# Attention scores with joined products, an earlier square root and another order of the projections, in a two-layer hybrid decoder on one core

## The chip, the core and the metric

The kernel runs on one core of a Trainium2 chip. The core has a matrix engine (TensorE, PE in the profile, with its weight loads as PEld), a vector engine (VectorE, DVE), an activation engine (ScalarE, ACT), GpSimd (POOL), and SyncE (SP), which here issues the loads. The metric is the device time of one execution in microseconds, and the median of several executions is compared.

## The reference

Two layers, 256 tokens, width 1024. A layer adds four things to the residual stream: half of a gated feed-forward network, a mixing block, half of a second feed-forward network, and a gated per-layer input. The change lies in the mixing block. From one normalized input it computes two branches and merges them:

```python
rx, rgate, q, k, v, f_logit, ga, gb = jnp.split(proj, split_idx, axis=-1)
rx = causal_dwconv(rx, conv_w[i], conv_b[i])
ya = rg_lru(rx, rg_wa[i], rg_ba[i], rg_wx[i], rg_bx[i], rg_lambda[i])
ya = (ya * jax.nn.gelu(rgate)) @ w_rnn_out[i]
yb = forgetting_attention(q, k, v, f_logit, f_b[i], q_norm[i], k_norm[i]) @ w_attn_out[i]
merged = jax.nn.sigmoid(ga + mb_a) * ya + jax.nn.sigmoid(gb + mb_b) * yb
x = x + merged @ w_o[i]
```

The recurrent branch `rg_lru` is a gated linear recurrence over the tokens: `a = exp(log_a)`, `u = sqrt(-expm1(2 log_a)) * (i * x)`, and `h[t] = a[t] h[t-1] + u[t]`. The attention has 8 heads of 128 dimensions and two blocks of 128 queries. To each score it adds a forget bias, the cumulated log forget gate of the query less that of the key, ahead of the causal mask and the softmax:

```python
s = jnp.einsum('bhqd,bhkd->bhqk', qb, kh).astype(jnp.float32) * scale
s = s + dqb[..., None] - dcum[:, :, None, :]
s = jnp.where(kpos[None, :] <= qpos[:, None], s, -jnp.inf)
pr = jax.nn.softmax(s, axis=-1).astype(vh.dtype)
```

The query's part of the bias is the same for all keys of a row.

## The kernel before

All activations lie with the features on the 128 partitions and the 256 tokens along the row. Every float32 operand of a large product is split into a high part, rounded to the matrix engine's fp32r format, and a low part, the rest. A product of two such operands takes three fp32r products: high times high, high times low and low times high.

**Weights.** The class `Weights` walks a plan, a list of loads in the order of their use. `_emit` issues a load on SyncE (1 MB, three raw buffers) and splits it in units of mostly 128x1024: ScalarE writes the high part (L95), VectorE the low part (L96). `next` hands out a unit and keeps four further ones split ahead (`ahead=4`, five buffers).

**Order.** The program is written once in a wished order; the framework's scheduler then orders each engine's instructions by a simulated timeline and by program order. Buffers of one tag form a ring. Small pieces of work are put off with `defer` and are taken up by `tick`, one step at a time, between products.

**The mixing block `mix`** goes through these stages:

1. Eight products for the recurrent input (`rx_post`): each is scaled by the norm and convolved over four tokens.
2. Values and forget logits (`v`), eight weight units. Between them `gates(m)` runs the products of the recurrence's two gates, with the follow-up steps `s1` (decay, its square) and `s2` (the square under the root in `tq`, the input in `xc`).
3. Queries and keys: four groups of four units, `qk_group(cb, w)`, `cb` being the half of the heads and `w` query or key. In `during0`, which runs after each unit of the first two groups, the last three `gates` and the generator `forget` are put in. `forget` computes the log forget gate, cumulates it with a triangular product into `dps` and splits it. After the second group come `drain` and `root`: one square root over all eight tiles (L570) and a tiny exponential that brings back the other activation table (L572).
4. In `during1`, after each unit of the third group, two calls of `scan` (multiply L575, recurrence L576). In the fourth group the first steps of attention start.
5. Twenty-four `filler` projections of 24 products of 256 columns each (L304 to L306): eight for the gelu gate (`f < KT`), eight for merge gate A, eight for merge gate B. A gelu filler has five VectorE operations behind it (L759, L763, L767, L768 and the split), a merge gate filler one (L759). The fillers use a ring of four PSUM banks ("mm"); their evictions take buffers from a ring of twelve ("w").
6. The merge: per pair of output tiles two products with `wro` (tiles `ya`) and two with `wao` (tiles `yb`), then the output projection.

**Attention** has four steps per head, put into slots that `attend(i)` runs. Slots 0 to 7 belong to the units of groups three and four, slots 8 to 31 to the 24 fillers. Head h starts at slot 4 + (5h+1)//2, and each step comes a slot later than the one before. `step_a` transposes queries and keys (L693), splits them into five buffers of a ring of five ("aq"), one of them a bias operand that ScalarE makes for each head (L702). `step_b` makes the scores in one PSUM bank: for the first query block three products over 128 keys and a bias product (L711), for the second the same over 256 keys. The bias product has rows for the high and low part of the query's bias and of the key's. Then come the masked minimum (L715), the exponential (L717) and the division (L719, L721). `step_c` transposes the probabilities (L729) and splits them, `step_d` multiplies by the values (L739, L741) and splits the result into `ot`. PSUM banks of attention form a second ring of four ("at").

Of the kernel before, what the change touches and what calls it, by code (L numbers as in the profile page):

```python
# [16 lines left out]
P = 128  # L17
# [3 lines left out]
S = 256  # L21
# [23 lines left out]
WARM = 9  # L45
MF, MA, MB, MO = 6, 8, 2, 6


# [71 lines left out]
def trunk(ctx: ExitStack, tc: tile.TileContext, head, xT, pT, vec, w1i, w1o, wf, wqk, wv, wg, wro, wao, wo, w2i, w2o,  # L120
# [39 lines left out]
    for l in range(DEPTH):  # L160
        plan += [(w1i[l, j], [1024, 1024]) for j in range(2 if l == 0 else 0, FT)]
        plan += [(w1o[l, m, :, h * 1408:(h + 1) * 1408], [768, 640]) for m in range(KT) for h in range(2)]
        plan += [(wf[l, 0, c], [1024, 1024]) for c in range(4)]
        plan += [(wv[l, c], [4 * VC, 4 * VC]) for c in range(4)]
        plan += [(wqk[l, qk, cb, hf], [1024, 1024]) for cb in range(2) for qk in range(2) for hf in range(2)]
        plan += [(wf[l, f, c], [1024, 1024]) for f in (1, 2, 3) for c in range(4)]
        plan += [(wrao, [1024, 1024]) for c in range(4) for wrao in (wro[l, c], wao[l, c])]
        plan += [(wo[l, c], [1024, 1024]) for c in range(4)]
        plan += [(w2i[l, j], [1024, 1024]) for j in range(FT)]
        plan += [(w2o[l, m, :, h * 1408:(h + 1) * 1408], [768, 640]) for m in range(KT) for h in range(2)]  # L170
        plan += [(wpg[l, c], [1024, 1024]) for c in range(4)]
# [30 lines left out]

    acol = cp.tile([P, NH], F32, name="acol")
    mcol = cp.tile([P, NH], F32, name="mcol")
    grp = cp.tile([P, 4], F32, name="grp")
    sel = cp.tile([P, 3], F32, name="sel")
    lfh = cp.tile([P, TT, P], F32R, name="lfh")
# [26 lines left out]
    def constants():  # L234
# [12 lines left out]
        yield  # L247
        V.tensor_tensor(out=acol, in0=ident[:, 0:NH], in1=ident[:, 32:32 + NH], op=ALU.add)
        V.tensor_tensor(out=mcol, in0=ident[:, 64:64 + NH], in1=ident[:, 96:96 + NH], op=ALU.add)
        V.tensor_scalar(out=mcol, in0=mcol, scalar1=-1.0, scalar2=None, op0=ALU.mult)  # L250
        yield
        for g in range(4):
            V.tensor_reduce(out=grp[:, g:g + 1], in_=ident[:, 32 * g:32 * g + 32], axis=AX.X, op=ALU.add)
        yield
        V.tensor_tensor(out=sel[:, 0:1], in0=grp[:, 1:2], in1=grp[:, 3:4], op=ALU.add)
        V.tensor_scalar(out=sel[:, 0:1], in0=sel[:, 0:1], scalar1=-1.0, scalar2=None, op0=ALU.mult)
        V.tensor_tensor(out=sel[:, 1:2], in0=grp[:, 0:1], in1=grp[:, 1:2], op=ALU.add)
        V.tensor_tensor(out=sel[:, 2:3], in0=grp[:, 2:3], in1=grp[:, 3:4], op=ALU.add)
        yield
# [243 lines left out]
    def mix(l, n, wgp):  # L503
# [42 lines left out]
        tq = big([P, KT, S], F32, "tq")  # L546

        def gates(m):
            ps = two[m % 2]("g")
# [14 lines left out]
            def s2():  # L564
                V.scalar_tensor_tensor(out=tq[:, m], in0=a2, scalar=1.0, in1=th, op0=ALU.add, op1=ALU.mult)
                V.scalar_tensor_tensor(out=xc[:, m], in0=thi, scalar=1.0, in1=xc[:, m], op0=ALU.add, op1=ALU.mult)
            defer(s1, s2)

# [5 lines left out]
        def scan(m):  # L574
            V.tensor_tensor(out=tq[:, m], in0=tq[:, m], in1=xc[:, m], op=ALU.mult)  # L575
            V.tensor_tensor_scan(out=xc[:, m], data0=at[:, m], data1=tq[:, m], initial=0.0, op0=ALU.mult, op1=ALU.add)  # L576
# [30 lines left out]

        dc = kp.tile([P, S], F32R, name=nm("dc"), tag="dc", bufs=1)
        dk = kp.tile([P, S], F32R, name=nm("dk"), tag="dk", bufs=1)

        def forget():
# [4 lines left out]
            for t in range(TT):  # L616
                oh = lfh[:, t].rearrange("p (g c) -> p g c", g=4)[:, :, 0:NH]
                ol = lfl[:, t].rearrange("p (g c) -> p g c", g=4)[:, :, 0:NH]
                V.tensor_copy(out=oh, in_=lf3[:, t].to_broadcast([P, 4, NH]))
                V.tensor_tensor(out=ol, in0=lf3[:, t].to_broadcast([P, 4, NH]), in1=oh.bitcast(F32), op=ALU.subtract)  # L620
            yield
# [7 lines left out]
            A.activation(out=dh, in_=dps[:, 0:S], func=AF.Copy)  # L629
            V.scalar_tensor_tensor(out=dc, in0=dh.bitcast(F32), scalar=sel[:, 0:1], in1=dps[:, 0:S], op0=ALU.mult,  # L630
                                   op1=ALU.add)
            V.tensor_scalar(out=dk, in0=dc.bitcast(F32), scalar1=sel[:, 1:2], scalar2=sel[:, 2:3], op0=ALU.mult,
                            op1=ALU.add)

# [45 lines left out]
        root()  # L680

# [5 lines left out]
        def step_a(h):  # L687
# [3 lines left out]
            for w in range(2):  # L691
                for t in range(TT):
                    T.transpose(ps[:, (w * TT + t) * P:(w * TT + t + 1) * P], qk[cb][:, w, t, hh * P:(hh + 1) * P], ident)  # L693
            s["q"] = qh, ql = awork(S, "aq", 5), awork(S, "aq", 5)
# [6 lines left out]
            V.scalar_tensor_tensor(out=kl, in0=ps[:, S:], scalar=g, in1=kh.bitcast(F32), op0=ALU.mult, op1=ALU.subtract)  # L701
            A.activation(out=s["b"], in_=dc.bitcast(F32), func=AF.Identity, scale=mcol[:, h:h + 1], bias=acol[:, h:h + 1])  # L702

        def step_b(h):
            s = st[h]
            (qh, ql), (kh, kl), bl = s["q"], s["k"], s["b"]
            ps = atbank("s")
            for t, o, nk in ((0, 0, P), (1, P, S)):
                q = slice(t * P, (t + 1) * P)
                mm3(ps[:, o:o + nk], qh[:, q], ql[:, q], kh[:, 0:nk], kl[:, 0:nk], True, False)  # L710
                T.matmul(ps[:, o:o + nk], lhsT=bl[:, q], rhs=dk[:, 0:nk], start=False, stop=True)  # L711
            sv = pr = awork(384, "pr", 2, F32)
            mx, rs = small(TT, "mx", "sa"), small(TT, "rs", "sa")
            for t, o, nk in ((0, 0, P), (1, P, S)):
                V.tensor_tensor_reduce(out=sv[:, o:o + nk], in0=ps[:, o:o + nk], in1=mask[:, S - nk:S], scale=1.0,  # L715
                                       scalar=3e38, op0=ALU.add, op1=ALU.min, accum_out=mx[:, t:t + 1])
# [318 lines left out]
```

## Time and profile before

| what | value |
|---|---|
| median of 3 runs | 1322.99 us (1322.97 to 1323.11) |
| profiled execution, its own time | 1323.63 us |
| its span, first to last instruction | 1321.8 us |
| instructions | 22442 |
| granted TensorE clock, mean | 0.997 |
| PE busy | 1311.8 us |
| DVE busy | 1076.1 us |
| ACT busy | 815.5 us |

A line of the timeline gives the start in us from the span's beginning, the duration, the engine, the line of the program, the operation and the tile written and tiles read, with partitions and elements. Matrix products are pipelined: their durations overlap, and the distance between two starts is what a product costs. A line of the groups gives a count, the busy time, the mean duration in ns, then the idle time of the engine ahead of such instructions and what ended it. A line of the windows gives for a stretch its length and the busy time of each engine.

### The profile page before, as it was taken

How to read it: one execution, taken by the hardware profiler on the slowest of the kernel's cores; microseconds unless marked ns; L12 is line 12 of the kernel's file. 1: busy time of each engine (PE TensorE's matmuls, PEld its weight loads, DVE VectorE, ACT ScalarE, POOL GpSimd, SP SyncE). 2: the span in 40 equal slices, each digit the busy share in tenths (PEclk: the TensorE clock that was granted, in tenths of full speed). 3: DMA queues.
4: the chain of work that ended last, by engine and by line, in shares of the span. 5: the costliest groups of instructions: out<-in, count | busy, mean ns of one | idle time of the engine just before them, and what ended most of it. 6: DMA issues, size and time to landing. Idle time of an engine off the chain costs nothing.

```text
span 1321.8 us, 22442 instructions
## 1 busy us (share of the span) xinstructions
PE 1311.8 (99%) x8610; PEld 1197.7 (91%) x8610; DVE 1076.1 (81%) x2142; ACT 815.5 (62%) x1470; POOL 34.1 (3%) x43
## 2 busy tenths in 40 slices
PE   9999999999999999999999999999999999999997
PEld 8888899889999888889988888998999998888897
DVE  7998769899757899876789877698997678988756
ACT  6665656868655666565566555578677556655653
POOL 1000000020000000000000000000200000000000
PEclk9999999999999999999999999999999999999998
DMA  8654665445435555456545546644543455554650
GB/s 292 243 179 160 212 225 193 158 164 175 151 128 191 196 189 189 162 184 231 187 165 192 188 153 212 241 161 159 193 166 128 161 190 191 192 191 142 213 187 33
DMA packets 37259, 240.21 MB, mean 182 GB/s; under 512 B 4128, under 2 KB 4768, under 8 KB 14368
## 3 DMA queue, kind: packets, MB, share of 16 engines
q1 hardware_dynamic: 36720, 238.25, 51.3%
q8 instruction: 68, 1.11, 0.3%
q10 hardware_dynamic: 432, 0.52, 0.1%
q14 instruction: 39, 0.32, 0.1%
HBM read 237.71 MB, written 1.05 MB: 181 GB/s over the span
## 4 chain that ended last, share of the span: by engine, by line
PE 99%; DMA 0%; DVE 0%; ACT 0%; SPq 0%; POOLq 0%; issue 0%; DVEq 0%
PE mm L347 20%; PE mm L345 11%; PE at L347 11%; PE at L345 6%; PE f L304 3%; PE f L305 3%; PE f L306 3%; PE qk L309 2%; PE qk L311 2%; PE qk L310 2%; PE mm L306 2%; PE mm L304 2%; PE mm L305 2%; PE ya L347 2%; PE mm L344 2%; PE at L344 2%
## 5 line engine op out<-in xcount | busy, mean ns | idle before, releaser
L95 ACT ACTIVATE wh<-wr 128x1024 fp32r<-128x1024 f32 (+2 forms) x476 | 467.4, 986 | 308.0 <-PE mm L347 90.8
L96 DVE TENSOR_TENSOR wl<-wr,wh 128x1024 fp32r<-128x1024 f32 (+2 forms) x476 | 537.7, 1132 | 142.3 <-ACT wh L95 136.9
L347 PE MATMUL mm<-h,wh 128*128 128x512 f32 x616 | 219.2, 394 | 0.0
L347 PE MATMUL at<-h,wh 128*128 128x512 f32 x616 | 218.4, 394 | 0.0
L345 PE MATMUL mm<-h,wl 128*128 128x256 f32 x704 | 182.4, 281 | 0.0
L345 PE MATMUL at<-h,wl 128*128 128x256 f32 x704 | 181.7, 281 | 0.3 <-DVE wl L96 0.2
L347 PE MATMUL mm<-f,wh 128*128 128x512 f32 x504 | 176.8, 394 | 0.0
L345 PE MATMUL mm<-f,wl 128*128 128x256 f32 x528 | 144.0, 280 | 0.0
L345 PEld LDWEIGHTS at<-h,wl 128*128 128x128 f32 x704 | 131.8, 188 | 8.8 <-DVE wl L96 0.8
L345 PEld LDWEIGHTS mm<-h,wl 128*128 128x128 f32 x704 | 131.8, 188 | 7.8 <-DVE wl L96 0.4
L347 PEld LDWEIGHTS mm<-h,wh 128*128 128x128 f32 x616 | 115.6, 188 | 22.5
L347 PEld LDWEIGHTS at<-h,wh 128*128 128x128 f32 x616 | 114.9, 188 | 21.9
L347 PEld LDWEIGHTS mm<-f,wh 128*128 128x128 f32 x504 | 94.4, 188 | 20.8
L304 PE MATMUL f<-h,wh 128*128 128x256 f32 x384 | 108.6, 283 | 0.0
L306 PE MATMUL f<-h,wl 128*128 128x256 f32 x384 | 108.4, 282 | 0.0
L305 PE MATMUL f<-h,wh 128*128 128x256 f32 x384 | 108.4, 282 | 0.0
L345 PEld LDWEIGHTS mm<-f,wl 128*128 128x128 f32 x528 | 99.4, 188 | 2.1
L305 PEld LDWEIGHTS f<-h,wh 128*128 128x128 f32 x384 | 72.3, 188 | 0.1
L304 PEld LDWEIGHTS f<-h,wh 128*128 128x128 f32 x384 | 72.3, 188 | 0.1
L306 PEld LDWEIGHTS f<-h,wl 128*128 128x128 f32 x384 | 72.4, 189 | 0.0
L381 ACT ACTIVATE sum<-mm 128x256 f32<-128x256 f32 x112 | 40.2, 376 | 49.3 <-PE mm L347 49.3
L382 DVE TENSOR_TENSOR sum<-mm,sum 128x256 f32<-128x256 f32 x112 | 44.9, 417 | 15.0 <-ACT sum L381 15.0
(291 smaller groups left out, 2857.6 us busy)
## 6 DMA issues: line engine op xcount, KB each, us to landing
wr<-in_w2i SPq DMA_DIRECT2D x44, 1024.0 KB, 4.8
wr<-in_w1i SPq DMA_DIRECT2D x41, 1024.0 KB, 4.8
wr<-in_wf SPq DMA_DIRECT2D x32, 1024.0 KB, 4.8
wr<-in_w1o SPq DMA_DIRECT2D x32, 704.0 KB, 4.0
wr<-in_w2o SPq DMA_DIRECT2D x32, 704.0 KB, 4.0
wr<-in_wqk SPq DMA_DIRECT2D x16, 1024.0 KB, 4.8
wr<-in_wv SPq DMA_DIRECT2D x8, 1032.0 KB, 4.9
wr<-in_wro SPq DMA_DIRECT2D x8, 1024.0 KB, 4.8
```

The source lines that it names most:

```text
L95: self.nc.scalar.activation(out=hi[:, c], in_=src[:, c], func=AF.Copy)
L96: self.nc.vector.tensor_tensor(out=lo[:, c], in0=src[:, c], in1=hi[:, c].bitcast(F32), op=ALU.subtract)
L304: T.matmul(ps, lhsT=wh, rhs=xh, start=first, stop=False)
L305: T.matmul(ps, lhsT=wh, rhs=xl, start=False, stop=False)
L306: T.matmul(ps, lhsT=wl, rhs=xh, start=False, stop=last)
L309: T.matmul(ps, lhsT=xh, rhs=wh, start=first, stop=False)
L310: T.matmul(ps, lhsT=xh, rhs=wl, start=False, stop=False)
L344: T.matmul(ps, lhsT=wh, rhs=t, start=True, stop=False, skip_group_check=True)
L345: T.matmul(ps[:, 0:S], lhsT=wl, rhs=t[:, 0:S], start=False, stop=False, skip_group_check=True)
L347: T.matmul(ps, lhsT=wh, rhs=t, start=False, stop=last, skip_group_check=True)
L381: A.activation(out=o, in_=ps[:, S:], func=AF.Copy)
L382: V.tensor_tensor(out=o, in0=ps[:, 0:S], in1=o, op=ALU.add)
```

## The change

The change has six parts.

- **Scores.** The high and low part of a head's key lie side by side in one buffer `ak`. Six products take the place of eight. Three run the second block's queries over 256 keys. One runs the first block's high queries over the high and the low key at once, 2 x 128 columns, into two pieces of the bank; one adds the first block's low queries. One product of 384 columns adds the bias to both blocks. VectorE adds the extra piece of the first block to the mask (`m0`, from the ring "w") ahead of the masked minimum.
- **Bias.** Only the key's part of the forget bias is added. `dk` holds its high and low rows over 256 keys and once more over the first 128. The weights of the bias product are one column of the selection matrix `pick`, read 128 times. The tile `dc`, the per-head bias operand on ScalarE, and the constants `acol`, `mcol`, `grp` and `sel` go; `neglo` and `pick` come.
- **Square root.** `root` moves from behind the second q/k group to the second unit of that group. The steps put off are taken up until all eight tiles are ready. `forget` is put off two units later.
- **Scans.** One scan follows each unit from there on, instead of two after each unit of the third group. Its multiplication stays behind the VectorE instruction written before it.
- **Projections in turn.** Two gelu fillers, then two of merge gate A, four times over; merge gate B last as before. The weights' plan follows that order.
- **Attention.** Its slots start at 8 (`AT0`) instead of 4.

```diff
-        plan += [(wf[l, f, c], [1024, 1024]) for f in (1, 2, 3) for c in range(4)]
+        plan += [(wf[l, f, c], [1024, 1024]) for c in range(4) for f in (1, 2)]
+        plan += [(wf[l, 3, c], [1024, 1024]) for c in range(4)]
...
+        V.tensor_tensor(out=pick, in0=ident[:, 0:NH], in1=ident[:, 32:32 + NH], op=ALU.add)
+        V.tensor_reduce(out=neglo, in_=ident[:, 32:64], axis=AX.X, op=ALU.add)
+        V.tensor_scalar(out=neglo, in0=neglo, scalar1=-1.0, scalar2=None, op0=ALU.mult)
...
         def scan(m):
-            V.tensor_tensor(out=tq[:, m], in0=tq[:, m], in1=xc[:, m], op=ALU.mult)
+            tc.keep_in_program_order(V.tensor_tensor(out=tq[:, m], in0=tq[:, m], in1=xc[:, m], op=ALU.mult))
...
-            V.scalar_tensor_tensor(out=dc, in0=dh.bitcast(F32), scalar=sel[:, 0:1], in1=dps[:, 0:S], op0=ALU.mult,
-                                   op1=ALU.add)
-            V.tensor_scalar(out=dk, in0=dc.bitcast(F32), scalar1=sel[:, 1:2], scalar2=sel[:, 2:3], op0=ALU.mult,
-                            op1=ALU.add)
+            for o, n_ in ((0, S), (S, P)):
+                V.scalar_tensor_tensor(out=dk[:, o:o + n_], in0=dh[:, 0:n_].bitcast(F32), scalar=neglo,
+                                       in1=dps[:, 0:n_], op0=ALU.mult, op1=ALU.add)
...
-                if w == 0 and u == 0:
+                if w == 0 and u == 2:
                     defer_gen(forget())
                 tick(2)
+                if w == 1 and u == 1:
+                    while len(ready) < KT:
+                        tick()
+                    root()
+                if w == 1 and u > 1:
+                    scan(u - 2)
...
         drain()
-        root()
...
-            s["k"] = kh, kl = awork(S, "aq", 5), awork(S, "aq", 5)
-            s["b"] = awork(S, "aq", 5)
+            s["q"] = qh, ql = awork(S, "aq", 2), awork(S, "aq", 2)
+            s["k"] = kk = kp.tile([P, 2, S], F32R, name=nm("ak"), tag="ak", bufs=1)
...
-            A.activation(out=s["b"], in_=dc.bitcast(F32), func=AF.Identity, scale=mcol[:, h:h + 1], bias=acol[:, h:h + 1])
...
-            for t, o, nk in ((0, 0, P), (1, P, S)):
-                q = slice(t * P, (t + 1) * P)
-                mm3(ps[:, o:o + nk], qh[:, q], ql[:, q], kh[:, 0:nk], kl[:, 0:nk], True, False)
-                T.matmul(ps[:, o:o + nk], lhsT=bl[:, q], rhs=dk[:, 0:nk], start=False, stop=True)
+            mm(slice(0, S), qh[:, q1], kk[:, 1], start=True)
+            mm(slice(0, S), qh[:, q1], kk[:, 0])
+            mm(slice(0, S), ql[:, q1], kk[:, 0])
+            mm(slice(S, 2 * S), qh[:, q0], kk[:, :, q0])
+            mm(slice(S, S + P), ql[:, q0], kk[:, 0, q0])
+            mm(slice(0, S + P), pick[:, h:h + 1].to_broadcast([P, P]), dk, stop=True)
...
+            m0 = work(s="m0")
+            V.tensor_tensor(out=m0[:, q0], in0=ps[:, S + P:], in1=mask[:, q1], op=ALU.add)
+            for t, o, nk, pc, mk in ((0, 0, P, slice(S, S + P), m0[:, q0]), (1, P, S, slice(0, S), mask)):
...
-                slots[4 + (5 * h + 1) // 2 + i].append((f, h))
+                slots[AT0 + (5 * h + 1) // 2 + i].append((f, h))
...
-                if w == 0:
-                    scan(2 * u)
-                    scan(2 * u + 1)
+                if 4 * w + u < KT - 2:
+                    scan(4 * w + u + 2)
...
-        for f in range(3 * KT):
+
+        turns = [f + m for m in range(0, KT, 2) for f in (0, 1, KT, KT + 1)] + list(range(2 * KT, 3 * KT))
+        for i, f in enumerate(turns):
             filler(f)
-            attend(KT + f)
+            attend(KT + i)
```

More of the change, by code (lines that the diff above doesn't have):

```diff
@@ L46 @@
 MF, MA, MB, MO = 6, 8, 2, 6
+AT0 = 8
 class Weights:
@@ L201, in trunk @@
     tri = cp.tile([P, S], F32R, name="tri")
[L203 to L206, printed above, removed]
+    neglo = cp.tile([P, 1], F32, name="neglo")
+    pick = cp.tile([P, NH], F32R, name="pick")
     lfh = cp.tile([P, TT, P], F32R, name="lfh")
@@ L247, in constants @@
         yield
[L248 to L258, printed above, removed]
+        V.tensor_tensor(out=pick, in0=ident[:, 0:NH], in1=ident[:, 32:32 + NH], op=ALU.add)
+        V.tensor_reduce(out=neglo, in_=ident[:, 32:64], axis=AX.X, op=ALU.add)
+        V.tensor_scalar(out=neglo, in0=neglo, scalar1=-1.0, scalar2=None, op0=ALU.mult)
         yield
@@ L546, in mix @@
         tq = big([P, KT, S], F32, "tq")
+        ready = []
         def gates(m):
@@ L566, in s2 @@
                 V.scalar_tensor_tensor(out=xc[:, m], in0=thi, scalar=1.0, in1=xc[:, m], op0=ALU.add, op1=ALU.mult)
+                ready.append(m)
             defer(s1, s2)
@@ L605, in mix @@
             tick(2)
-        dc = kp.tile([P, S], F32R, name=nm("dc"), tag="dc", bufs=1)
-        dk = kp.tile([P, S], F32R, name=nm("dk"), tag="dk", bufs=1)
+        dk = kp.tile([P, S + P], F32R, name=nm("dk"), tag="dk", bufs=1)
         def forget():
@@ L616, in forget @@
             for t in range(TT):
[L617 to L620, printed above, removed]
+                oh = lfh[:, t].rearrange("p (g c) -> p g c", g=4)[:, 0:2, 0:NH]
+                ol = lfl[:, t].rearrange("p (g c) -> p g c", g=4)[:, 0:2, 0:NH]
+                V.tensor_copy(out=oh, in_=lf3[:, t].to_broadcast([P, 2, NH]))
+                V.tensor_tensor(out=ol, in0=lf3[:, t].to_broadcast([P, 2, NH]), in1=oh.bitcast(F32), op=ALU.subtract)
             yield
@@ L693, in step_a @@
                     T.transpose(ps[:, (w * TT + t) * P:(w * TT + t + 1) * P], qk[cb][:, w, t, hh * P:(hh + 1) * P], ident)
-            s["q"] = qh, ql = awork(S, "aq", 5), awork(S, "aq", 5)
-            s["k"] = kh, kl = awork(S, "aq", 5), awork(S, "aq", 5)
-            s["b"] = awork(S, "aq", 5)
+            s["q"] = qh, ql = awork(S, "aq", 2), awork(S, "aq", 2)
+            s["k"] = kk = kp.tile([P, 2, S], F32R, name=nm("ak"), tag="ak", bufs=1)
+            kh, kl = kk[:, 0], kk[:, 1]
             g = gqk[:, l:l + 1]
@@ L701, in step_a, with mm @@
             V.scalar_tensor_tensor(out=kl, in0=ps[:, S:], scalar=g, in1=kh.bitcast(F32), op0=ALU.mult, op1=ALU.subtract)
-            A.activation(out=s["b"], in_=dc.bitcast(F32), func=AF.Identity, scale=mcol[:, h:h + 1], bias=acol[:, h:h + 1])
         def step_b(h):
             s = st[h]
-            (qh, ql), (kh, kl), bl = s["q"], s["k"], s["b"]
+            (qh, ql), kk = s["q"], s["k"]
+            q0, q1 = slice(0, P), slice(P, S)
             ps = atbank("s")
-            for t, o, nk in ((0, 0, P), (1, P, S)):
-                q = slice(t * P, (t + 1) * P)
-                mm3(ps[:, o:o + nk], qh[:, q], ql[:, q], kh[:, 0:nk], kl[:, 0:nk], True, False)
-                T.matmul(ps[:, o:o + nk], lhsT=bl[:, q], rhs=dk[:, 0:nk], start=False, stop=True)
+            def mm(o, w, r, start=False, stop=False):
+                T.matmul(ps[:, o], lhsT=w, rhs=r, start=start, stop=stop, skip_group_check=True)
+            mm(slice(0, S), qh[:, q1], kk[:, 1], start=True)
[4 more added lines that the diff above has]
+            mm(slice(0, S + P), pick[:, h:h + 1].to_broadcast([P, P]), dk, stop=True)
             sv = pr = awork(384, "pr", 2, F32)
             mx, rs = small(TT, "mx", "sa"), small(TT, "rs", "sa")
-            for t, o, nk in ((0, 0, P), (1, P, S)):
-                V.tensor_tensor_reduce(out=sv[:, o:o + nk], in0=ps[:, o:o + nk], in1=mask[:, S - nk:S], scale=1.0,
+            m0 = work(s="m0")
+            V.tensor_tensor(out=m0[:, q0], in0=ps[:, S + P:], in1=mask[:, q1], op=ALU.add)
+            for t, o, nk, pc, mk in ((0, 0, P, slice(S, S + P), m0[:, q0]), (1, P, S, slice(0, S), mask)):
+                V.tensor_tensor_reduce(out=sv[:, o:o + nk], in0=ps[:, pc], in1=mk, scale=1.0,
                                        scalar=3e38, op0=ALU.add, op1=ALU.min, accum_out=mx[:, t:t + 1])
```

## The prediction

> **What bounds the kernel now.** I read the page's busy times and chain first.
>
> ```profile
> span 1321.8 us, 22442 instructions
> PE 1311.8 (99%) x8610; PEld 1197.7 (91%) x8610; DVE 1076.1 (81%) x2142; ACT 815.5 (62%) x1470; POOL 34.1 (3%) x43
> PE 99%; DMA 0%; DVE 0%; ACT 0%; SPq 0%; POOLq 0%; issue 0%; DVEq 0%
> ```
>
> The chain that ended last is TensorE throughout: 99% of it, and no other engine reaches 1%. So only two things can move the end: the time that TensorE needs for its own products, and idle time that the change opens on it. Work on the other engines counts only where it makes TensorE wait.
>
> Next I need what a product costs. The busy durations overlap, so I take distances between starts, from the timeline of PE. A long run of 512-wide products, 78 of them, and a run of 256-wide fillers, 88 of them, each by first and last row:
>
> ```profile
> 261.05 0.45 PE L309 MATMUL qk<-wh,h 128*128 128x512 f32 x1
> ...
> 278.93 0.40 PE L311 MATMUL qk<-wh,h 128*128 128x512 f32 x1
> ```
>
> (278.93 - 261.05)/77 is 0.232 us. The fillers run from 309.27, in the next fence, to 319.55: 10.28/87 is 0.118 us. Then one head's scores, all but their first product:
>
> ```profile
> 308.24 0.36 PE L305 MATMUL f<-h,wh 128*128 128x256 f32 x1
> 308.44 0.22 PE L305 MATMUL s<-aq,aq 128*128 128x128 f32 x1
> 308.50 0.27 PE L306 MATMUL s<-aq,aq 128*128 128x128 f32 x1
> 308.61 0.28 PE L711 MATMUL s<-dk,aq 128*128 128x128 f32 x1
> 308.72 0.34 PE L304 MATMUL s<-aq,aq 128*128 128x256 f32 x1
> 308.90 0.29 PE L305 MATMUL s<-aq,aq 128*128 128x256 f32 x1
> 309.02 0.28 PE L306 MATMUL s<-aq,aq 128*128 128x256 f32 x1
> 309.14 0.29 PE L711 MATMUL s<-dk,aq 128*128 128x256 f32 x1
> 309.27 0.28 PE L306 MATMUL f<-h,wl 128*128 128x256 f32 x1
> ...
> 319.55 0.28 PE L306 MATMUL f<-h,wl 128*128 128x256 f32 x1
> ```
>
> The 128-wide products are half as wide as the 256-wide ones and are not half as dear. Inside the run they stand 0.11 apart. The first seems to cost only 0.06 (308.44 to 308.50), but the first wide one then takes 0.18 instead of 0.118 (308.72 to 308.90), so the 0.06 is paid back. Together the seven take 0.83 us, which is 3 x 0.110 + 4 x 0.118 = 0.80 and a little. The weight loads of the same stretch say why:
>
> ```profile
> 308.45 0.19 PEld L306 LDWEIGHTS s<-aq,aq 128*128 128x128 f32 x1
> 308.56 0.19 PEld L711 LDWEIGHTS s<-dk,aq 128*128 128x128 f32 x1
> 308.67 0.19 PEld L304 LDWEIGHTS s<-aq,aq 128*128 128x128 f32 x1
> 308.78 0.19 PEld L305 LDWEIGHTS s<-aq,aq 128*128 128x128 f32 x1
> ```
>
> Loads never follow one another faster than 0.11 us. A 256-wide product covers the next load (0.118), a 128-wide one (about 0.06 of streaming) does not. A narrow product therefore costs a load, 0.110 us.
>
> **The change, part by part.**
>
> *Score products.* Before, a head has four narrow products and four 256-wide ones: 4 x 0.110 + 4 x 0.118 = 0.912 us. After, it has four of 256 (three for the second query block, one that runs the first block's queries over both halves of the key's split), one of 128 and one of 384 that adds the bias. The columns stay 1536; two loads go. The 384-wide product lies halfway between the 256 and the 512 rows: 0.175. So 4 x 0.118 + 0.110 + 0.175 = 0.757, and 0.155 less per head. Eight heads in two layers: **16 x 0.155 = 2.48 us, all on the chain**.
>
> Three things in it the trace doesn't show. The joined product reads its columns in two strips: from 0.118, as one 256-wide product, to 0.220, as two narrow ones; I take 0.118, since the column count is what the rows follow; the other end gives back 16 x 0.102 = 1.6. The 384-wide price has the 256 and the 512 rows as ends, 16 x 0.057 = 0.9 either way; I keep the middle. The bias product's weights are one column read 128 times: if that load were free, the narrow product before it would cost 0.06 and not 0.11, another 0.8 gained; if it took as long as two loads, 16 x 0.110 = 1.8 is lost. I take one load, the only size there is among the rows for a 128-column fp32r operand.
>
> By the Trainium skill, page "TensorE: Matmul & The Clock Gate", section "Back-to-back issue gap", an isolated product takes N/2.4 + 2.5 ns, 56 ns for 128 columns and 109 for 256. By that rule the joining would save next to nothing, since the columns stay: an estimate from that page of 4 x 56 + 4 x 109 = 660 ns before and 655 after, 0.1 us in all. The narrow rows above, 0.11 apart, do not follow it.
>
> *The addition m0 and the bias column.* VectorE gains one 128-wide addition out of PSUM per head. ScalarE loses the activation that made the bias operand.
>
> ```profile
> L702 ACT ACTIVATE aq<-dc,acol,mcol 128x256 fp32r<-128x256 f32 x16 | 9.6, 599 | 0.0
> L715 DVE CUSTOM_DVE_ANT_0 pr<-s,mask 128x128 f32<-128x128 f32 x16 | 4.5, 284 | 1.4 <-PE s L711 1.4
> L701 DVE SCALAR_TENSOR_TENSOR aq<-tr,gqk,aq 128x256 fp32r<-128x256 f32 x16 | 7.6, 474 | 0.0
> L721 DVE TENSOR_SCALAR pr<-pr,rs 128x256 f32<-128x256 f32 x16 | 5.5, 346 | 0.0
> L732 DVE TENSOR_TENSOR pl<-pt,ph 128x384 fp32r<-128x384 f32 x16 | 8.8, 551 | 0.7 <-ACT ph L731 0.7
> L759 DVE TENSOR_TENSOR g<-f,RB 128x256 f32<-128x256 f32 x48 | 20.1, 418 | 12.0 <-PE f L306 11.4
> L763 DVE SCALAR_TENSOR_TENSOR sq<-sq,g 128x256 f32<-128x256 f32 x16 | 6.6, 414 | 0.0
> L96 DVE TENSOR_TENSOR wl<-wr,wh 128x1024 fp32r<-128x1024 f32 x332 | 404.3, 1221 | 84.7 <-ACT wh L95 83.1
> ```
>
> The nearest row to m0 is the masked minimum on 128 columns, 0.284; the ends are nothing and 0.418. That is 4.5 us more VectorE and 9.6 us less ScalarE over the run, none of it on the chain as long as the fillers' products stand in front of TensorE. The forget preparation changes by two small VectorE operations a layer; its first reader is the first head's score product, so the second block's q/k products cover it. The setup loses eight small VectorE operations net, all in the time in which VectorE waits for the first weights to land, so nothing is gained.
>
> *Square root ahead, scans paced.* The same ScalarE block (table load, root, reload) stands half a q/k group earlier, ahead of weight splits and q/k squares. VectorE's timeline shows what the block does now:
>
> ```profile
> 265.18 1.23 DVE L96 TENSOR_TENSOR wl<-wr,wh 128x1024 fp32r<-128x1024 f32 x1 [0.63 <-ACT wh L95]
> 268.49 2.44 DVE L575 TENSOR_TENSOR tq<-tq,xc 128x256 f32<-128x256 f32 x7 [2.09 <-ACT tq L570]
> ...
> 274.37 1.20 DVE L96 TENSOR_TENSOR wl<-wr,wh 128x1024 fp32r<-128x1024 f32 x1
> ```
>
> Root and scans leave 9.2 us between two weight splits, and TensorE stood through that in the run of 78 quoted above without a gap: four units ahead, 12 x 0.232 = 2.8 us each, are 11 us of cover. Spread out, the gap gets shorter. Cost: nothing; with that cover gone it would be up to those 9.2 us a layer.
>
> *Projections in turn, weights in that order.* The same 24 fillers and the same 1 MB loads on SP's queue in the order in which they are used, so each load keeps its place before its use: nothing on TensorE. On VectorE the gelu fillers (two more multiplications and a split than a gate filler) no longer come eight in a row.
>
> *Attention four slots later.* This moves when its products appear, not their number. Here lies the risk, since VectorE is full just there (columns: window, sum, then busy us of PE, PEld, DVE, ACT):
>
> ```profile
> 260.00:288.00 28.00, 28.00 (x127) 22.71 (x126) 24.25 (x48) 18.84 (x25) 6.32 (x4) 1.00 0.42 151
> 288.00:312.00 24.00, 24.00 (x201) 23.74 (x200) 23.99 (x55) 17.95 (x39) 2.92 (x2) 1.00 0.61 209
> 312.00:336.00 24.00, 24.00 (x207) 24.00 (x206) 22.03 (x50) 17.42 (x38) 0.00 (x0) 1.00 0.45 159
> 336.00:360.00 24.00, 24.00 (x209) 24.00 (x208) 16.94 (x42) 15.94 (x38) 0.00 (x0) 1.00 0.42 156
> ```
>
> The pace of attention shows in the first transpose of the probabilities of heads 0, 2, 4 and 6:
>
> ```profile
> 301.96 0.27 PE L729 MATMUL pt<-ident,pr 128*128 128x128 f32 x1
> ...
> 332.13 0.27 PE L729 MATMUL pt<-ident,pr 128*128 128x128 f32 x1
> ...
> 345.13 0.28 PE L711 MATMUL s<-dk,aq 128*128 128x256 f32 x1
> ...
> 350.67 0.27 PE L729 MATMUL pt<-ident,pr 128*128 128x128 f32 x1
> 350.78 0.27 PE L693 MATMUL tr<-ident,qk 128*128 128x128 f32 x1
> ...
> 369.54 0.27 PE L729 MATMUL pt<-ident,pr 128*128 128x128 f32 x1
> ```
>
> Two heads take 30.2, 18.5 and 18.9 us. Five fillers and two heads are TensorE work of 120 x 0.118 + 2 x 2.2 = 18.6 us (2.2: scores 0.76 and thirteen further products at 0.109 to 0.118). So attention keeps pace except in the first pair, when VectorE is at 100%. In the new order a filler brings on average 1.22 + (5 x 0.416 + 0.418)/2 = 2.47 us of VectorE in the first sixteen (the weight split, then five operations like L759 and L763, or one). A head brings 3 x 0.418 + 0.474 + 2 x 0.284 + 0.346 + 0.28 + 0.551 and a short reciprocal, 3.6 us, and over two and a half fillers 1.4 each. That is 3.9 against 2.83 + 2.2/2.5 = 3.7 us of TensorE: over by 0.2 us a filler, some 3 us until the gelu fillers are through, and then far under. Fillers can run ahead by their four PSUM banks, 4 x 2.83 = 11.3 us. 3 is under 11.3, so I put TensorE's idle time at nothing.
>
> *Sum.* On the profiled run: span 1321.8 - 2.48 = 1319.3, and with the 1.8 us by which its time (1323.63) exceeds its span, 1321.1. The median shown, 1322.99, is 0.6 below that run; the same step from it gives **1320.5 us**.
>
> **The rivals.**
>
> *Part of it eaten.* TensorE idles 0.3 to 1.2 us a layer at one of the new joints. For it: the order of work is new everywhere in this stage. Against it: no gap there now. 1321 to 1323.
>
> *Attention holds up the fillers: slower.* m0 takes its buffer from the ring of twelve that the fillers' evictions use; buffers of one ring appear to be given in program order (head 5's transposes start at 350.78, right behind head 4's, though head 4's last score product, which frees their operands, started at 345.13). Then a filler behind a late head cannot evict, and after four banks TensorE stops. It decides once attention is over 11.3 us late. If one pair again takes 30.2 instead of 18.6, 11.6 us, behind a first head that starts some 4 us late, 15.6 - 11.3 = 4.3 us are lost per layer: 1320.5 + 8.6 = 1329. Against it: the first pair was slow under eight gelu fillers in a row and q/k work left over from the scans, and both are spread now.
>
> *Narrow products are not bound by loads,* the page's rule as a mechanism: with 0.06 for each, before is 4 x 0.06 + 4 x 0.118 = 0.712, after 0.707, and the time stays at 1322.9. Against it, the rows at 0.11.
>
> *The stretched column, or the two strips, cost more:* 2.48 - 1.8 or - 1.6, so 1322.2. Nothing for it in the trace.
>
> *The stretched column loads for next to nothing:* 2.48 + 0.8, so 1319.7.
>
> **How the numbers follow.** No idle time, 1320.5, holds 0.60; eaten in part 0.11; held up 0.15; rule of columns 0.04; dearer operand 0.05; cheaper load 0.05. A measurement tells this kernel from no change at about 0.2%, 2.65 us, so below 1320.34 is faster and above 1325.64 slower. My sum ends 0.17 short of the first, and the 512- and 256-wide rows leave it some 0.3 of play: of the 0.60 I give 0.20 to faster. Faster 0.20 + 0.05 = 0.25. Slower: the held-up case but for its mild end, 0.14. The rest, 0.61, is the same. The range, 1319.6 to 1324.6, takes in the cheaper load below and the eaten and dearer cases above, and leaves out most of the held-up one; the likeliest case alone spans 1320.0 to 1321.0.
>
> **What would show it.** Score products: 6 per head, PE instructions down by 32; starts of one head's group about 0.76 us from first to the next filler, the narrow one still 0.11, the bias product about 0.175 behind its start. PE's idle time between 10 and 1310 us still nothing, VectorE under 100% between 288 and 312, the last head's output products no later against the merge than now. Wrong if a filler or the merge shows idle time on PE released by VectorE, or if the bias product's load stands over 0.11 from its neighbour.

## The result, and the profile after the change

The changed kernel takes 1335.28 us (median of 5 runs, 1333.04 to 1336.28); the kernel before takes 1323.11 beside it (5 runs). The ratio is 1.009, with an interval of 1.0077 to 1.0104: slower by 12.2 us. The forecast was 1320.5, in a range up to 1324.6. The profiled run took 1336.18, its span is 1334.5. The five executions differ in the mean granted clock too: 0.995 in the two longest (1336.18 and 1336.28 us), 0.997 in the next two, 0.998 in the shortest (1333.04).

The page of the changed kernel, its span, busy times and chain:

```profile
span 1334.5 us, 22395 instructions
PE 1313.9 (98%) x8578; PEld 1197.0 (90%) x8578; DVE 1080.4 (81%) x2150; ACT 808.4 (61%) x1454; POOL 40.1 (3%) x43
PE 94%; DVE 3%; ACT 1%; issue 0%; POOL 0%; DMA 0%; POOLq 0%; DVEq 0%
```

TensorE has 32 instructions fewer, as the change says. But the chain, which was TensorE's to 99%, now has 5 points of it elsewhere, 3 of them VectorE. The waits of PE say where (engine, tile and line that wait, what they wait for; us in total, times, longest):

```profile
PE f L296 <- DVE g L766: 5.3, 4, 1.4
PE ya L336 <- DVE g L766: 3.6, 2, 1.8
...
PE s L710 <- DVE s L654: 0.6, 2, 0.4
```

A filler's product (`f`, L296) and the merge's first product (`ya`, L336) wait for a PSUM bank, which the eviction of an earlier filler (`g`, L766) gives free. That is 8.9 us in six waits, three in each layer; in the kernel before there was none of them. The windows of the mixing block in the first layer (window, sum, then busy us of PE, PEld, DVE, ACT and POOL, granted clock, DMA share, GB/s) give the stage:

```profile
288.00:312.00 24.00, 23.64 (x197) 23.23 (x196) 23.64 (x51) 14.87 (x29) 3.87 (x3) 1.00 0.59 216
312.00:336.00 24.00, 24.00 (x206) 23.99 (x205) 20.23 (x49) 15.95 (x36) 0.00 (x0) 1.00 0.38 137
336.00:360.00 24.00, 21.35 (x179) 20.84 (x178) 19.49 (x49) 15.72 (x36) 0.00 (x0) 1.00 0.42 138
360.00:386.00 26.00, 24.04 (x176) 22.75 (x175) 15.90 (x44) 14.32 (x32) 0.00 (x0) 0.93 0.31 117
```

TensorE had 24.00 of 24 us in the first three of these windows before; now it lacks 2.65 us between 336 and 360 and 1.96 behind that. VectorE is not what it lacks: between 336 and 360 VectorE is busy for 19.5 of 24 us. The two timelines of the first long gap show it. PE:

```profile
336.12 0.75 PE L710 MATMUL s<-ak,aq 128*128 128x256 f32 x5
336.71 0.39 PE L710 MATMUL s<-dk,pick 128*128 128x384 f32 x1
336.94 0.60 PE L691 MATMUL tr<-ident,qk 128*128 128x128 f32 x4
338.92 0.39 PE L296 MATMUL f<-h,wh 128*128 128x256 f32 x1 [1.38 <-DVE g L766]
```

And DVE over the same time, with its last eviction of a filler before that:

```profile
325.81 0.42 DVE L766 TENSOR_TENSOR g<-f,RB 128x256 f32<-128x256 f32 x1
...
333.88 1.23 DVE L97 TENSOR_TENSOR wl<-wr,wh 128x1024 fp32r<-128x1024 f32 x1
336.78 1.23 DVE L97 TENSOR_TENSOR wl<-wr,wh 128x1024 fp32r<-128x1024 f32 x1 [1.67 <-ACT wh L96]
337.92 0.28 DVE L720 TENSOR_TENSOR m<-s,mask 128x128 f32<-128x128 f32 x1
338.12 0.41 DVE L327 TENSOR_TENSOR ot<-o,ot 128x256 fp32r<-128x256 f32 x1
338.45 0.75 DVE L766 TENSOR_TENSOR g<-f,RB 128x256 f32<-128x256 f32 x2
```

The fillers whose sums `g` takes out of PSUM were computed before 336.12, ahead of the scores. From 325.81 to 338.45 VectorE evicted no filler at all, though it stood idle for 1.67 us up to 336.78, since its next instruction needed the high part of a weight unit. The evictions come behind `m` (L720), the addition `m0` of the head whose scores ended at about 337, and two of them come at once. So the eviction waits for the head, not because VectorE lacks time.

The time lies in the mixing block alone. From its first value product to its last output product it takes 236.5 us in the first layer against 230.1 before; what lies outside of it kept its length within 0.5 us. The saving forecast is 1.24 a layer, so 7.7 us a layer are lost. Idle time is 5.0 of that (0.36 ahead of the first head's scores, 1.38 and 1.27 at fillers, 0.14, 1.83 at the merge). Each of these gaps costs some 0.2 to 0.25 us more than its idle time, by starts (at 336.94 the four transposes need 4 x 0.109, so the filler could start at 337.38, 1.54 ahead of 338.92), about 1 us together. The rest is the clock behind the last gap, which the last section shows; this account is that of the profiled execution, one of the two longest.

### The profile page after: what moved, and what is told of

Its sections match the earlier page's. It is cut to its first block, busy times and chain, and to the rows that moved or that the text cites. A ratio compares the mean times of both kernels' runs of the same rounds, so it can differ in the third digit from the quotient of the medians.

```text
span 1334.5 us, 22395 instructions
## 1 busy us (share of the span) xinstructions
PE 1313.9 (98%) x8578; PEld 1197.0 (90%) x8578; DVE 1080.4 (81%) x2150; ACT 808.4 (61%) x1454; POOL 40.1 (3%) x43
## 4 chain that ended last, share of the span: by engine, by line
PE 94%; DVE 3%; ACT 1%; issue 0%; POOL 0%; DMA 0%; POOLq 0%; DVEq 0%
PE mm L339 19%; PE mm L337 11%; PE at L339 11%; PE at L337 6%; PE f L296 3%; PE f L297 3%; PE f L298 3%; PE mm L296 2%; PE mm L298 2%; PE mm L297 2%; PE ya L339 2%; PE mm L336 2%; PE at L336 2%; PE o L339 1%; PE pl L296 1%; PE pl L298 1%
## 5 line engine op out<-in xcount | busy, mean ns | idle before, releaser
L296 PE MATMUL f<-h,wh 128*128 128x256 f32 x384 | 109.1, 284 | 5.3 <-DVE g L766 5.3
L296 PEld LDWEIGHTS f<-h,wh 128*128 128x128 f32 x384 | 72.3, 188 | 6.3 <-DVE g L766 6.3
```

The source lines that it names most:

```text
L296: T.matmul(ps, lhsT=wh, rhs=xh, start=first, stop=False)
```

## The experiments

In all of them the time of the kernel before, taken on the same chip, lies between 1323.0 and 1323.5 us. The theory is the second rival of the prediction, "Attention holds up the fillers": `m0` takes its buffer from the fillers' ring `w`, buffers are given in program order, and a late head stops the fillers. Against it stand a shortage of buffers, attention being put too late, and another part of the change.

**e1: `m0` gets a ring of its own.**

```diff
-            m0 = work(s="m0")
+            m0 = awork(S, "m0", 1, F32)
```

> The changed kernel with one edit: m0 takes its buffer from a ring of its own (one buffer) instead of the fillers' ring w. Theory 'shared ring' (a filler written behind a late head cannot get its eviction buffer until that head's m0 has been given one, so four filled PSUM banks stop TensorE): the waits of the first filler product on the eviction of an earlier filler go, the idle 1.5 us behind the transposes of heads 4 and 6 and the 2 us ahead of the merge go with them, and the time is 1320.5 (1319.8 to 1321.5). Rival 'attention too late' (starting four slots later, with VectorE full, is itself what stops TensorE): the gaps stay or move into the merge, and the time stays above 1330.

Measured: 1321.74 us, ratio 0.999 (0.9981 to 1.0), 13.5 below the changed kernel and 0.2 above the range expected. All six long waits are gone. Of the mixing block only this wait of PE is left, and its place in the timeline follows:

```profile
PE s L710 <- DVE s L654: 0.6, 2, 0.3
```
```profile
295.60 0.59 PE L710 MATMUL s<-ak,aq 128*128 128x256 f32 x3 [0.34 <-DVE s L654]
```

One line of the change made it slow. The matrix products and the operations of VectorE and ScalarE are the same in number (x8578, x2150, x1454); the buffer differs, and with it the order in which VectorE gets its work: in e1 it evicts fillers at 330.24 and 333.76 us, ahead of the `m` of the same head at 334.76.

**e2: fourteen buffers in the shared ring, not twelve.**

```diff
-        return kp.tile([P, 256], dt, name=nm(s), tag="w", bufs=12)
+        return kp.tile([P, 256], dt, name=nm(s), tag="w", bufs=14)
```

> The changed kernel with fourteen instead of twelve buffers in the ring w. If the ring is simply too small by the one buffer that m0 holds, two more buffers bring the time to about 1320.5. If buffers are given in program order, so that the place of m0 in the order counts and not the number of buffers, the gaps stay and the time stays near 1335 (1331 to 1337).

Measured: 1334.86 us, ratio 1.0091 (1.0076 to 1.0106), with the same waits: `f` on `g` 5.3 us in four, `ya` on `g` 3.6 in two. So it isn't the number of buffers that counts. What is left is the order in which they are handed out; no run changes that order alone, but the evictions right behind `m` fit it.

**e3: attention four slots earlier, where it was before.**

```diff
-AT0 = 8
+AT0 = 4
```

> The changed kernel with attention's slots starting at 4 as before; m0 stays in the ring w. 'Shared ring': each head stands four fillers earlier in program order, but the fillers behind it now wait for it just as before; whether the head is done by then decides. With four slots more of a head's start against the fillers' some 0 to 5 us a layer are lost: 1320.5 to 1330. 'Attention too late': all the loss goes, 1320.5.

Measured: 1332.96 us, ratio 1.0079 (1.0062 to 1.0096). That is above the 1330 that I had put as the upper end: four slots win only 2.3 us. The gaps move from 339, 359 and 380 us to 327, 348 and 368; all three are now at fillers:

```profile
PE f L296 <- DVE g L766: 8.7, 6, 1.7
```

So the later start of attention is not the cause.

**e5 and e6: the ring alone, in the kernel before.** One column of the scores is copied into a buffer that nothing reads; everything else stays. e5 takes it from the shared ring, e6 from one of its own.

```diff
+            m0 = work(s="m0")                  # e5
+            m0 = awork(1, "m0", 1, F32)        # e6, in its place
+            V.tensor_copy(out=m0[:, 0:1], in_=ps[:, 0:1])
```

> The kernel before with one thing added: step_b takes a buffer from the fillers' ring w and copies one score column into it, which nothing reads. Everything else as before. VectorE gains 32 operations of some 0.16 us. 'Shared ring': in the kernel before, heads run about nine fillers behind their place in the program, while the ring then lets fillers run ahead by four banks only; TensorE gets idle time on fillers released by their evictions, as in the changed kernel, and the time rises to 1328 to 1340. If what stopped TensorE in the changed kernel was tied to its later slots or its order of projections: no change, 1323.1.

> The control to the run before it: the same copy into a buffer of a ring of its own. 'Shared ring': no change, 1323.1 (1322.8 to 1323.8), no idle time on TensorE between 10 and 1310 us. If the mere extra VectorE step in the chain of a head did it: slower like the run before it.

Measured: e5 1334.14 us, ratio 1.0083 (1.0068 to 1.0098); e6 1323.1, ratio 1.0 (0.999 to 1.001). The same sixteen copies of 0.15 us cost 11 us or nothing, by their buffer. The waits of PE in e5, and the first of them in its timeline, which again stands behind a head's last score product:

```profile
PE f L304 <- DVE g L761: 6.2, 4, 2.1
```
```profile
326.70 0.28 PE L711 MATMUL s<-dk,aq 128*128 128x256 f32 x1
329.10 0.39 PE L304 MATMUL f<-h,wh 128*128 128x256 f32 x1 [2.12 <-DVE g L761]
```

The kernel before already had its heads this late; it had nothing that tied the fillers to them. How late, can be counted: the fillers that TensorE has begun before a head's last score product, less those that the program puts ahead of it. In the first layer, with the heads counted from 0, these are 8.3 to 8.5 for heads 3 to 6 of the kernel before, without a gap. In the changed kernel, e3 and e5 no head gets above 4.0, which is the number of the fillers' PSUM banks: there TensorE stands instead. In e1 heads 3 to 7 are 3.1 to 4.1 late and in e7 5.9 to 8.0, and nothing stops.

**e4: the joined scores alone.** The kernel before, with the new scores, key bias and `m0` (in its own ring), and with the old place of root and scans, old order of projections, and attention where it was.

```diff
+            mm(slice(S, 2 * S), qh[:, q0], kk[:, :, q0])
+            mm(slice(0, S + P), pick[:, h:h + 1].to_broadcast([P, P]), dk, stop=True)
...
+            m0 = awork(S, "m0", 1, F32)
```

> The kernel before with the joined score products and the key-only bias alone, m0 in a ring of its own; root, scans, order of projections and slots as before. The sum of the prediction for the products alone: 16 x 0.155 = 2.48 us less, 1320.5 (1320.0 to 1321.2), no idle time on TensorE between 10 and 1310 us, the six products of a head 0.76 us apart from first to the next filler. If narrow products are not bound by their loads: 1323. If the stretched column or the joined strips cost more: 1321.5 to 1322.5.

Measured: 1328.93 us, ratio 1.0044 (1.0029 to 1.0058). I had expected the whole saving, 1320.5. The products are saved (x8578), but the time is 5.8 us above the kernel before, so with the saving some 8 us are lost; 5.9 of them are waits of the merge and the output projection that neither kernel had:

```profile
PE o L335 <- DVE sum L373: 2.6, 2, 1.3
PE ya L335 <- ACT wh L96: 1.8, 2, 0.9
PE ya L336 <- DVE wl L97: 1.5, 2, 0.8
```

The last head's transposes of the probabilities begin at 388.7 us in e4, at 385.0 in the kernel before and at 383.9 in e1; behind the merge's first product that is 17.9, 11.8 and 11.0 us. So the other parts of the change, which I had costed at nothing, do something. Three runs take them back one at a time from e1.

**e8: e1 with the old order of projections.**

```diff
-        turns = [f + m for m in range(0, KT, 2) for f in (0, 1, KT, KT + 1)] + list(range(2 * KT, 3 * KT))
+        turns = list(range(3 * KT))
```

(and the weight plan with it)

> The changed kernel with m0 in a ring of its own and the projections in their old order (eight gelu fillers in a row), root, scans and slots as changed. The run with the joined products alone lost some 7 us against the sum by waits in the merge. If the order of the projections is what keeps attention in time, this one loses as much or more: 1328 to 1334, with waits in the merge. If the spread root and scans do that: 1321.7, as with the projections in turn.

Measured: 1329.32 us, ratio 1.0046 (1.0031 to 1.0061), with the three waits of e4 at the same places. The projections in turn are worth 7.6 us once the scores are joined.

**e10: e1 with root, scans and forget preparation at their old places** (the scans' multiplication loses its fixed place, too).

```diff
-                if w == 1 and u == 1:
-                    while len(ready) < KT:
-                        tick()
-                    root()
...
+        root()
```

> The changed kernel with m0 in a ring of its own, and with root, scans and the forget preparation where they were before (root behind the second q/k group, two scans after each unit of the third). Projections in turn and slots from 8 stay. My account: the root and the scans were not on TensorE's chain and their place costs nothing as such: 1321.7 (1321 to 1322.5). Rival: bunched scans leave q/k work behind that makes the first heads late again: 1323 or more, with idle time on TensorE between 288 and 312 us.

Measured: 1323.77 us, ratio 1.0003 (0.9994 to 1.0012), 2.0 above e1 (on another chip; 1.7 by the kernel before beside each). My account missed: the time is the rival's. But the rival's reason doesn't show either, since TensorE has no idle time between 288 and 312 us. The lost time is one gap a layer, in the merge. PE of e10 in its timeline:

```profile
384.86 0.49 PE L731 MATMUL pt<-ident,pr 128*128 128x128 f32 x3
386.22 0.50 PE L336 MATMUL ya<-yr,wh 128*128 128x512 f32 x1 [0.87 <-ACT wh L96]
...
386.82 0.39 PE L336 MATMUL yb<-ot,wh 128*128 128x512 f32 x1
```

And ACT, which writes the weights' high parts:

```profile
382.33 1.07 ACT L96 ACTIVATE wh<-wr 128x1024 fp32r<-128x1024 f32 x1 [0.66 <-PE ya L339]
...
385.11 1.06 ACT L96 ACTIVATE wh<-wr 128x1024 fp32r<-128x1024 f32 x1 [1.72 <-PE ya L339]
```

ScalarE waited 1.72 us for a buffer that a `ya` product frees, and the next `ya` then waited for the unit. My reading: weight units are split in plan order, recurrent and attention by turns; while the last head is late, `yb` units fill the five buffers unread, and the `ya` products run out of units.

**e11: e4 with all recurrent products of the merge ahead of the attention's.** It tests that reading.

```diff
-        plan += [(wrao, [1024, 1024]) for c in range(4) for wrao in (wro[l, c], wao[l, c])]
+        plan += [(wro[l, c], [1024, 1024]) for c in range(4)] + [(wao[l, c], [1024, 1024]) for c in range(4)]
...
+        for m in range(KT):
+            ps = mmbank("ya")
+            unit(ps, yr)
+            pa.append(total(ps))
```

> The kernel before with the joined products alone (m0 in a ring of its own, all else in its old place) and one change in the merge: all eight products with the recurrent output weights come first, then the eight with the attention weights; the weights' plan follows. Same products. The run without that change took 1328.9, with 0.8 to 1.3 us gaps in the merge on weight splits. Theory 'late attention in the merge': the weight units for the attention products are given their buffers early and hold them until the last head is done, so the next recurrent units have none; with the recurrent products first, 16 us more work stands ahead of the first use of the last head, the gaps go, and the products' saving shows: 1320.6 (1320 to 1321.5). Rival: the gaps come from VectorE and ScalarE being busy, whatever the order: 1326 or more.

Measured: 1324.59 us, ratio 1.0011 (1.0002 to 1.002), 4.3 below e4, but 3.1 above the range expected. Both waits of `ya` are gone; the one of the output projection stays:

```profile
PE o L335 <- DVE sum L373: 2.8, 2, 1.4
```

So the reading fits the merge, and the rest of the expected saving didn't come. The last wait is in e4, e8 and e11, all with the joined scores and the old order of projections. It is in no run with the new order, and not in the kernel before, which has the old one; by what mechanism, no run shows.

**e7 and e9: e1 with attention from slot 4 and from slot 6.**

```diff
-AT0 = 8
+AT0 = 4        # e7; 6 in e9
```

> The changed kernel with m0 in a ring of its own and slots from 4 as before. In the own-ring run TensorE still lost 0.5 us per layer in front of the first head's scores, where VectorE had q/k work of the last group ahead of the key's split. Theory: with slots from 4 the first head's splits come earlier in program order, ahead of that work, and the whole 2.5 us show: 1320.6 (1320.2 to 1321.2). Rival: an earlier first head only moves the wait, or delays the q/k work behind it: 1321.7 or more.

> The changed kernel with m0 in a ring of its own and slots from 6. With slots from 8 TensorE lost 0.5 us per layer ahead of the first head's scores, with slots from 4 about 0.25 us on one filler's eviction in the same stretch, both where VectorE is at 100%. Between them the loss should be no larger: 1320.6 to 1321.7. If the place of the first head has nothing to do with it, 1321.7 as with 8.

Measured: e7 1321.6 us, ratio 0.9989 (0.9979 to 0.9998). The wait at the first head's scores is gone, but the whole 2.5 us don't show: the median is 0.4 above the range expected, little below e1. e9 1323.55, ratio 1.0 (0.9991 to 1.0009), with the merge's wait of e10 (0.87 us, once a layer); e9 is not between e7 and e1, and I missed it. The last head's first transposes of the probabilities begin 8.2 us behind the merge's first product in e7, 11.0 in e1, 12.7 in e9 and 12.7 in e10, and only the last two have the wait. So it seems to be the lateness of the last head that decides, and that doesn't follow the slot in a simple way.

**e12: e7 with the recurrent products first** (the edit of e11 on e7).

> The changed kernel with m0 in a ring of its own, slots from 4, and the same order of the merge as in the run before it. With slots from 4 there was no idle time in the merge already, so the order should win nothing here: 1321.2 to 1321.7, as without it. More than 0.5 us less would mean that the merge still cost something that the trace does not show as idle time.

Measured: 1321.06 us, ratio 0.9984 (0.9976 to 0.9993), the fastest of all, and below both kernels. It is a little under the range expected and 0.5 below e7, just at the bound that I had set; the profiled spans of the two are the same, 1319.3, so whether the order of the merge wins anything here stays open. Its page:

```profile
span 1319.3 us, 22356 instructions
PE 1308.7 (99%) x8578; PEld 1194.5 (91%) x8578; DVE 1082.2 (82%) x2150; ACT 808.7 (61%) x1454; POOL 36.1 (3%) x43
```

## Why the prediction was wrong, point by point

**What bounds the kernel:** right. The kernels differ by TensorE's own work, by TensorE standing, and by its clock; none differs by another engine's busy time.

**Score products: right in kind, a little too large in size.** Where nothing long stops TensorE, the time is 1.4 us (e7) and 2.0 us (e12) below the kernel before taken beside it; 2.48 was forecast. The mixing block, from its first value product to its last output product, takes 229.0 and 229.1 us in the two layers of e12, against 230.1 in both before: 1.0 to 1.1 less, where 1.24 was forecast. That the span of both profiles is the 1319.3 of the forecast is in part luck: of the 2.5 us to the 1321.8 before, 0.5 lie behind the last `fin` product, in the program's end (that product starts at 1313.25 before and at 1311.20 in e12). One head's group in e1, by PE's timeline:

```profile
375.99 0.69 PE L710 MATMUL s<-ak,aq 128*128 128x256 f32 x5
376.53 0.39 PE L710 MATMUL s<-dk,pick 128*128 128x384 f32 x1
376.76 0.28 PE L337 MATMUL ya<-yr,wl 128*128 128x256 f32 x1
```

It takes 0.77 us from 375.99 to 376.76, forecast about 0.76. The 384-wide product takes 0.23 here, with the 0.06 in it that the narrow one ahead of it defers, so some 0.17 to 0.18, forecast 0.175. Over the eight groups of e1 that stand unbroken it is 0.760 to 0.765 for the six; with 0.118 for each of the four and 0.109 for the narrow one, 0.18 is left for 384 columns. Inside the row of five, the product in two strips starts at 376.35 and the next one at 376.47, 0.12 apart as for plain 256 columns. The load of the column read 128 times starts at 376.47, 0.12 behind the load before it, and the next load at 376.58, 0.11 behind. So neither costs or saves anything that these rows show, and the prediction's sign against it, a load over 0.11 from its neighbour, was set without any play. (That loads never follow one another faster than 0.11 us holds for the rows shown; in the whole trace before, 26 of 8609 come sooner, at 0.06 to 0.10, most of them loads of transposes.) The rival that narrow products are not bound by loads would have saved nothing, and is out.

**The addition `m0`: size right, place wrong.** From the groups by line and form in e1:

```profile
L720 DVE TENSOR_TENSOR m<-s,mask 128x128 f32<-128x128 f32 x16 | 4.6, 285 | 1.6 <-PE s L710 1.6
```

285 ns, forecast 284. What it cost was its buffer: 13.5 us in the changed kernel, against 4.6 us of VectorE off the path.

**The step that failed** is "3 is under 11.3, so I put TensorE's idle time at nothing". The 11.3 was the right margin (the fillers do stop when their banks are full), the 3 was wrong. I worked it out as throughput: VectorE's work a filler less TensorE's. My reading is that a head is a chain: transposes, splits, scores, minimum, exponential, normalization, transposes again, each hop behind whatever the next engine is doing. With its own ring two heads take 21.6, 21.6 and 19.3 us in e1, by their first transposes of the probabilities at 306.8, 328.4, 350.0 and 369.3, not the 18.6 that TensorE's work gives, though VectorE is busy for only 20.3 of 24 us from 336 to 360. So in place of 3 us, heads 3 to 7 are 3.1 to 4.1 fillers late even with nothing tied, 3.1 x 2.83 = 8.8 to 4.1 x 2.83 = 11.6 us, about the whole 11.3. With the shared ring the heads get later still, since `m0` in turn waits for the fillers' evictions ahead of it in the ring (argued from the order). Measured is that head 2 is 3.0 fillers late in the changed kernel and 2.5 in e1, its first transpose at 331.1 and 328.4, and that head 3 has reached the limit of 4.0, where it is 3.1 late in e1; the first long gap of TensorE stands right behind that head's scores. A row to warn of it was among those quoted: 30.2 us for the first pair before. I explained it away by the gelu fillers.

**The held-up rival: right in its mechanism, too low in price.** It had 0.15 and 1329; measured is 1335. I priced one stall of 4.3 us a layer. There are three long ones, because lateness stays near the limit once it is reached (3.7 to 4.0 fillers for heads 3 to 7) and later heads stop the fillers again: 5.0 us idle a layer, about 1 for starting again, and some 1.7 of half clock.

**Root, scans and projections at nothing:** right as a cost, wrong as a worth. They take nothing, but without them the joined scores lose some 2 us (e10 against e1) and 7.6 (e8 against e1). I considered only what these moves might delay and not what the new scores would need. Why the joined scores bring the last head later in e4 stays open. One more short step on VectorE is not enough for it: in e6, with a copy of 0.15 us more in each head, the last head's first transposes begin at 384.5, 385.0 before. Nor is it that the operands of only one head fit: the ring of five before held the five buffers of one head, too.

**"VectorE under 100% between 288 and 312":** hardly. It is busy for 23.64 of 24 us in the changed kernel, and for all 24 in e1, where nothing stops the fillers:

```profile
288.00:312.00 24.00, 23.66 (x197) 23.21 (x196) 24.00 (x53) 15.45 (x30) 4.04 (x3) 1.00 0.59 223
...
336.00:360.00 24.00, 24.00 (x206) 23.99 (x206) 20.30 (x55) 16.37 (x38) 0.00 (x0) 1.00 0.39 137
```

VectorE is as good as full there, as before, and TensorE idles 0.34 us ahead of the first head.

**"Wrong if a filler or the merge shows idle time on PE released by VectorE":** this is what the waits of the changed kernel show, and the releaser named is the eviction, though what kept it, by e1, e5 and e6, was the ring from which the head's buffer came.

**"The last head no later against the merge":** holds, but says little. Its first transposes of the probabilities come 8.0 us behind the merge's first product in the changed kernel and 11.8 us before, since the merge was held up as well.

## What to carry to other kernels

A buffer for a new operation should not come from a ring that another, faster stream of work also draws on: if buffers are handed out in program order, the slow stream's place in the program becomes a barrier for the fast one, and two more buffers didn't help here (e2; e5 and e6 are a cheap test). Whether a stream falls behind is worked out hop by hop along its chain, and from how late it already is in the trace, not from the sums of busy time. A move that costs nothing may still carry what another part of the change needs, so parts are priced together, at the place with the least margin, here the merge.

## What the runs showed of the hardware

The clock of TensorE fell after a short pause. In the changed kernel PE stands for 1.83 us ahead of the merge; its timeline there:

```profile
377.53 0.39 PE L710 MATMUL s<-dk,pick 128*128 128x384 f32 x1
379.75 0.68 PE L336 MATMUL ya<-yr,wh 128*128 128x512 f32 x1 [1.83 <-DVE g L766]
...
381.29 0.63 PE L339 MATMUL ya<-yr,wh 128*128 128x512 f32 x1
...
381.93 0.63 PE L339 MATMUL ya<-yr,wh 128*128 128x512 f32 x1
...
383.62 0.40 PE L339 MATMUL ya<-yr,wh 128*128 128x512 f32 x1
...
383.97 0.39 PE L339 MATMUL ya<-yr,wh 128*128 128x512 f32 x1
```

A 512-wide and a 256-wide product together take 0.64 us from 381.29 to 381.93 and 0.35 from 383.62 on. The window from 379.9 to 383.3 has a granted clock of one half:

```profile
379.90:383.30 3.40, 3.40 (x12) 2.92 (x13) 2.05 (x10) 2.41 (x8) 0.00 (x0) 0.50 0.28 111
```

3.4 us at half speed lose 1.7 us of work, an estimate from these two numbers. It occurs once more in the second layer, from 1038.7, after 1.80 us of idle time; gaps of 1.3 to 1.4 us in the same run, and of 1.7 in e3, are not followed by it. In e5 one gap of 2.1 us is followed by it and another of 2.1 is not; in e2 one of 1.82 is and one of 1.80 is not. So a pause of this length decides it only in part. The spread of the changed kernel's five executions fits such stretches: two of them take 0.0026 off the mean clock over 1334 us, which is about the step from 0.998 in the shortest execution to 0.995 in the two longest. What the 0.997 of the other two means can't be told, since the end of every run is at half clock as well, for a length that differs (8.6 us in the profile before, 5.0 in e6). The Trainium skill, page "TensorE: Matmul & The Clock Gate", section "What's actually happening", gives half clock after at least one idle window of about 3.4 us. The 3.4 us of half clock agree with that length; the pause of 1.8 us ahead of it is shorter than the page's.
